# Fourteen early expert products from whole operands, token-by-token one-hots and ten whole closing blocks in a one-core encoder step

## The chip, the core and the metric

The kernel runs on one core of a Trainium2 chip. A core has five engines that run beside each other, each with its own instruction queue: TensorE (PE, matrix products; its weight loads are listed apart as PEld), VectorE (DVE), ScalarE (ACT), GpSimd (POOL) and SyncE (SP, which only issues transfers here). The metric is the device time in microseconds of one execution: the median of several runs.

## The reference, cut to what matters

The program is one layer of an encoder for two groups of tokens that share all weights: 512 prompt tokens and 128 sample tokens, 1024 features each. First comes a mixing part (gated spatial unit, differential attention, gated DeltaNet), then PEER, a retrieval of single-neuron experts. Only PEER is touched:

```
q = (h @ w_query).reshape(n, 8, 2, 128)
s = einsum('nhpd,hpkd->nhpk', q, sub_keys)        # 8 heads, 2 halves, 128 keys each
top_s, top_i = top_k(s, 16)
cand = top_s[:, :, 0, :, None] + top_s[:, :, 1, None, :]
best_s, best_c = top_k(cand.reshape(n, 8, 256), 16)
ids   = i1 * 128 + i2                              # 128 of 16384 experts per token
gates = softmax(best_s)
act = gelu(einsum('nkd,nd->nk', expert_u[ids], h))
out = einsum('nk,nkd->nd', gates * act, expert_v[ids])
x = layer_norm(alpha * x + gate2 * out)
```

## The kernel before

The 640 tokens are five tiles of 128: tiles 0 to 3 are the prompt, tile 4 the samples. The two halves of PEER use the experts in two ways.

Tiles 0 to 2 (384 tokens) go densely through all experts, in 128 blocks of 128 experts. For block n the **u product** is a 128 x 384 table of first products (24 matmuls), ACT makes gelu of it into a tile `ga` (L1539), DVE multiplies it by that block's dense gates `gt` (L1706), and the **v product** adds the block's share of the output into six PSUM banks (18 matmuls). Tiles 3 and 4 fetch the rows of their own experts by indirect DMA, one row per token at a time (512 fetches in all, issued by POOL at L1675), and DVE either dots the row with the token (L1684) or adds it, weighted, into the output (L1690).

Operands are kept in pairs: the value rounded to a shorter type (`uh`, `vh`, `wh`, `h2h`, written by ACT, or by POOL for h) and the remainder (`ul`, `vl`, `wl`, `h2l`, written by DVE). Each product is three passes: high x high, high x low, low x high. Hence 24 = 3 x 8 matmuls in a u product and 18 = 3 x 6 in a v product.

PEER runs in these stages, each of which appears below by its time in the trace:

- the selection of the sample tile, which lies beside the end of the mixing part
- **d_prompt** (660 to 801 us): query products on PE for the 512 prompt tokens, scores, and the two top-16 selections on DVE (L1309 to L1343). Beside it run the u products of blocks 0 to 7 (`prefill`, LEAD = 8), woven in by `lanes`, a merger that takes the next piece of whichever list is least far ahead by the costs that the pieces yield
- **d_decode** (801 to 842 us): DVE turns the selected positions into expert numbers and gates (L1354 to L1389)
- **table** (842 to 990 us): 48 groups of 8 tokens build the dense gates. Per group DVE compares (`ob`, L1612; `o2`, L1615) and multiplies (`o1`, L1616, for five tokens, printed `o`); ACT multiplies the other three (`o1a`, L1614); PE does 8 matmuls into bank `sa`; ACT copies twice into `stg` (L1621), which goes to DRAM (`gdense`)
- the **loop** over m = 0 to 127 (from 990 us): iteration m does the v product of block m and the u product of block n = m + 8, prepares the operands of the next ones, and issues and consumes a share of the fetches that `goal(m)` sets, so that the last one is consumed in iteration END = 118. The order of the work on each queue is as written: `tick` pieces lie between `v_hi`, `g_hi`, `u_split`, `g_lo`, `v_lo`
- the **tail** (from 2051 us): residual, gating and layer norm of the tiles (`base` L1736 and L1739, `final_stats` L1744, `final` L1752 to L1756), placed in iterations 121, 122 and 123 for tiles 3 and 4, and the last three v blocks (LAST = 3), which multiply v by the gate first (L1697) and are added at L1849

## Time and profile before

| | us |
|---|---|
| median of 3 runs | 2128.05 (2126.98 to 2131.91) |
| profiled execution: its own time | 2136.78 |
| profiled execution: span of the trace | 2134.7 |
| PE busy in the span | 1918.1 (90%) |
| DVE busy | 1765.8 (83%) |
| ACT busy | 707.1 (33%) |
| POOL busy | 803.9 (38%) |

The profiled execution took 8.7 us more than the median, 0.4%. In the span's 40 equal slices TensorE's granted clock is 0.9 or full nearly everywhere; from the slice that begins at about 1014 us on, the DMA engines are busy at nine tenths or more until the tail, at 382 to 409 GB/s. Times in the rows below are counted from the start of the span; an item `x8` is a run of eight instructions of one kind, and the time in square brackets is how long the engine stood idle before it and for whom.

### The profile page before, as it was taken

The numbers are of one execution on the slowest core, as the hardware profiler recorded it, in microseconds if no ns is written. First come the engines' busy times: TensorE is split into PE (matmuls) and PEld (weight loads), VectorE is DVE, ScalarE is ACT, GpSimd is POOL, SyncE is SP. The second block draws the span as 40 slices with busy tenths as digits, with TensorE's granted clock in tenths as the row PEclk, the third lists the DMA queues.
The fourth block names the chain that finished last, engine by engine and source line by source line (L and its number), as shares of the span: only waits on it lengthen the run. The fifth ranks groups of instructions, "written<-read, shape, count | busy, mean of one in ns | idle before, by whom it ended". The sixth has DMA issues, their size and how long they took to land.

```text
span 2134.7 us, 32342 instructions
## 1 busy us (share of the span) xinstructions
PE 1918.1 (90%) x11979; PEld 1621.0 (76%) x11979; DVE 1765.8 (83%) x3923; ACT 707.1 (33%) x1257; POOL 803.9 (38%) x637
## 2 busy tenths in 40 slices
PE   5899979988969972999999999999999999999983
PEld 3888956664658871998998888888888888888862
DVE  5753057666898999886999989999999999999987
ACT  2331133332124321886333333333333333333320
POOL 1322122110004201000666666665666666665610
PEclk7999989999989995999999999999999999999986
DMA  7345276523333202567999999999999999999961
GB/s 272 123 177 188 81 237 213 183 93 140 120 136 119 100 20 89 169 189 228 387 409 409 406 382 390 400 399 398 394 399 407 398 408 388 397 395 397 384 235 69
DMA packets 211655, 572.58 MB, mean 268 GB/s; under 512 B 20351, under 2 KB 89471, under 8 KB 206634
## 3 DMA queue, kind: packets, MB, share of 16 engines
q1 hardware_dynamic: 129674, 293.43, 38.0%
q0 software_dynamic: 73728, 268.47, 31.9%
q10 hardware_dynamic: 8096, 8.63, 1.2%
q8 instruction: 94, 1.54, 0.3%
q14 instruction: 63, 0.52, 0.1%
HBM read 535.57 MB, written 34.36 MB: 267 GB/s over the span
## 4 chain that ended last, share of the span: by engine, by line
PE 32%; DVE 21%; issue 18%; POOL 18%; DMA 7%; ACT 3%; ACTq 0%; POOLq 0%; SPq 0%; DVEq 0%
PE mm L188 15%; POOL rows L1675 9%; POOL acc L1675 9%; PE sa L188 7%; PE a L188 3%; PE g L188 3%; ACT uh L243 1%; DVE vl L1702 1%; DMA rows<-in_v_dram,idq 1%; DMA acc<-in_v_dram,ids 1%; DVE acc L1690 1%; DVE acc L1684 1%; DVE ycs L1690 1%; DVE rows L1684 1%; DVE ul L244 1%
## 5 line engine op out<-in xcount | busy, mean ns | idle before, releaser
L1709 ACT CAST wh<-ga 128x384 fp32r<-128x384 f32 x128 | 65.7, 514 | 715.6 <-DVE ga L1706 715.6
L188 PE MATMUL mm<-h2h,uh 128*128 128x384 f32 x1024 | 203.8, 340 | 12.7 <-ACT uh L243 12.2
L188 PEld LDWEIGHTS mm<-h2h,uh 128*128 128x128 f32 x1024 | 179.2, 188 | 35.8 <-ACT uh L243 28.3
L244 DVE TENSOR_TENSOR ul<-ur,uh 128x1024 fp32r<-128x1024 f32 x127 | 155.6, 1225 | 55.5 <-ACT uh L243 55.5
L188 PE MATMUL mm<-h2l,uh 128*128 128x384 f32 x1024 | 199.6, 336 | 0.0
L188 PE MATMUL mm<-h2h,ul 128*128 128x384 f32 x1024 | 199.4, 336 | 0.0
L1675 POOL DMA_INDIRECT acc<-in_u_dram,idq x65 | 83.2, 1280 | 272.3 <-DVE act_q L1684 193.2
L188 PE MATMUL sa<-vl,wh 128*128 128x512 f32 x384 | 160.5, 418 | 25.6 <-DVE vl L1702 25.6
L188 PEld LDWEIGHTS mm<-h2h,ul 128*128 128x128 f32 x1024 | 180.6, 188 | 0.0
L188 PEld LDWEIGHTS mm<-h2l,uh 128*128 128x128 f32 x1024 | 180.5, 187 | 0.0
L188 PE MATMUL sa<-vh,wh 128*128 128x512 f32 x384 | 153.7, 400 | 23.1 <-ACT wh L1709 19.2
L1702 DVE TENSOR_TENSOR vl<-vr,vh 128x1024 fp32r<-128x1024 f32 x128 | 156.2, 1221 | 0.7 <-ACT vh L1699 0.7
L188 PE MATMUL sa<-vh,wl 128*128 128x512 f32 x384 | 152.4, 397 | 0.0
L1699 ACT CAST vh<-vr 128x1024 fp32r<-128x1024 f32 x128 | 133.0, 1039 | 30.3 <-DVE vr L1697 21.4
L243 ACT CAST uh<-ur 128x1024 fp32r<-128x1024 f32 x128 | 133.9, 1047 | 15.2 <-PE mm L188 15.2
L188 PE MATMUL sa<-o,o 128*128 128x128 f32 x480 | 118.7, 408 | 12.2 <-DVE o L1616 12.2
L188 PEld LDWEIGHTS sa<-vl,wh 128*128 128x128 f32 x384 | 73.3, 191 | 61.7 <-DVE vl L1702 49.4
L188 PEld LDWEIGHTS sa<-o,o 128*128 128x128 f32 x480 | 95.2, 209 | 20.7 <-DVE o L1616 12.6
L244 POOL TENSOR_TENSOR wlo<-raw,whi 128x2048 fp32r<-128x2048 f32 (+1 forms) x12 | 55.2, 4597 | 139.8 <-ACT whi L243 108.8
L188 PE MATMUL tp<-vh,wh 128*128 128x512 f32 x256 | 102.2, 399 | 0.0
L188 PE MATMUL tp<-vl,wh 128*128 128x512 f32 x256 | 102.0, 399 | 0.0
L1675 POOL DMA_INDIRECT acc<-in_v_dram,ids x65 | 82.2, 1265 | 52.0 <-DVE ycs L1690 46.2
(474 smaller groups left out, 4688.3 us busy)
## 6 DMA issues: line engine op xcount, KB each, us to landing
ur<-in_uT_dram SPq DMA_DIRECT2D x128, 512.0 KB, 6.7
vr<-in_v_dram SPq DMA_DIRECT2D x128, 512.0 KB, 6.6
raw<-in_wada_dram SPq DMA_DIRECT2D x24, 1024.0 KB, 6.6
gdense<-stg SPq DMA_DIRECT2D x12, 2048.0 KB, 8.7
gt<-gdense SPq DMA_DIRECT2D x31, 768.0 KB, 9.4
ck<-in_ckT_dram SPq DMA_DIRECT2D x32, 512.0 KB, 5.7
cv<-in_cv_dram SPq DMA_DIRECT2D x32, 512.0 KB, 4.5
wqr<-in_wq_dram SPq DMA_DIRECT2D x32, 512.0 KB, 3.2
```

The costliest lines, as they stand in the source:

```text
L188: PE.matmul(out, lhsT=lhsT, rhs=rhs, start=start, stop=stop, **kw)
L243: S.copy(out=hi, in_=raw)
L244: e_lo.tensor_tensor(out=lo, in0=raw, in1=hi.bitcast(F32), op=ALU.subtract)
L1675: G.indirect_dma_start(out=r, out_offset=None, in_=I["v"] if k else I["u"], in_offset=bass.IndirectOffsetOnAxis(ap=who[t][0][:, s:s + 1], ...
L1684: V.tensor_tensor_reduce(out=r, in0=r, in1=h2, scale=1.0, scalar=0.0, op0=ALU.mult, op1=ALU.add, accum_out=act[:, s:s + 1])
L1690: V.scalar_tensor_tensor(out=facc[t], in0=r, scalar=act[:, s:s + 1], in1=facc[t], op0=ALU.mult, op1=ALU.add)
L1699: S.copy(out=vs[n][0], in_=w)
L1702: V.tensor_tensor(out=vs[n][1], in0=vls.pop(n), in1=vs[n][0].bitcast(F32), op=ALU.subtract)
L1709: S.copy(out=ws[n][0], in_=ga)
```

## The change

- **Early u products from whole operands.** NPRE = 14 blocks are now computed ahead of the loop, in the order 8 to 13, then 0 to 7. Eight of them (8 to 13, 0, 1) are woven beside d_decode, six (2 to 7) beside the table; d_prompt runs alone. They use the 32-bit u block and the 32-bit h of tiles 0 to 2 directly (no `uh`/`ul`): 24 matmuls of 128 columns each. For this `h2f` keeps h of the three tiles, copied by DMA into buffers named `acc`, which later serve the fetches. Blocks 8 to 13 store their `ga` to DRAM (`gad`), and iterations 0 to 5 of the loop load them back; those iterations have no u product and no `u_split`. The split of block 14 is done by POOL.
- **One-hots token by token.** `o1` is laid out as 5 rows of 128 instead of 128 rows of 5. PE now reads it contiguously; DVE writes it with a step of 512 bytes between neighbours.
- **Whole operands at the end.** For blocks from WHOLE = 118 on, v and `ga` are used as they are: no `vh`, `vl`, `wh`, `wl`, and 6 matmuls of 512 columns in place of 18.
- **Pacing.** END is 121, `goal` gives the first six iterations half a share of fetches, and `base`/`final` of tiles 3 and 4 lie in iterations 122 to 124.

```diff
@@ -27,6 +27,7 @@
 NP = 512
 ND = 384
 LEAD = 8
+NPRE = 14
 NB = 8
 TS = 16
 PAST = 1024
@@ -1288,11 +1289,16 @@
     cx = ExitStack()
     oc = Out(cx)
 
+    h2f = {}
+
     def h2_tile(t):
         hm = T(oc.p, [P, 8, P], "hm")
         oc.feat(t, hm)
         r = slice(t * P, (t + 1) * P)
         split(hm, h2h[:, :, r], h2l[:, :, r], G)
+        if t < 3:
+            h2f[t] = T(ac, [P, D], "acc", bufs=4)
+            nc.scalar.dma_start(out=h2f[t].rearrange("p (c t) -> p c t", c=8), in_=hm)
         if t == 3:
             for hf in range(2):
                 pt = bank("tp")
@@ -1540,16 +1546,29 @@
 
     uls, uhs, gas = {}, {}, {}
 
-    def prefill():
-        uls[0] = u_load(0)
-        uls[1] = u_load(1)
-        uhs[0] = u_split(uls.pop(0), G)
-        yield 0
-        for n in range(LEAD):
-            uls[n + 2] = u_load(n + 2)
-            uhs[n + 1] = u_split(uls.pop(n + 1), V)
-            u_gelu(n, u_block(n))
-            yield 5
+    gad = T(dp, [NPRE - LEAD, P, ND], "gad")
+    early = list(range(LEAD, NPRE)) + list(range(LEAD))
+
+    def prefill(k0, k1):
+
+        for k in range(k0, k1):
+            n = early[k]
+            if k + 2 < NPRE:
+                uls[early[k + 2]] = u_load(early[k + 2])
+            w = uls.pop(n)
+            gas[n] = T(eu, [P, ND], "ga", bufs=LEAD + 1)
+            pa = bank("mm")
+            for t in range(3):
+                for dc in range(8):
+                    mm(pa[:, t * P:(t + 1) * P], w[:, dc, :], h2f[t][:, dc * P:(dc + 1) * P], dc == 0, dc == 7)
+            u_gelu(n, pa)
+            if n >= LEAD:
+                nc.sync.dma_start(out=gad[n - LEAD], in_=gas.pop(n))
+            yield 5.4
+        if k1 == NPRE:
+            for n in range(NPRE, NPRE + 2):
+                uls[n] = u_load(n)
+            uhs[NPRE] = u_split(uls.pop(NPRE), G)
 
     def d_decode():
         for t in range(4):
@@ -1558,8 +1577,11 @@
         V.scalar_tensor_tensor(out=i1f[:, 3, :], in0=i1f[:, 3, :], scalar=128.0, in1=i2f[:, 3, :], op0=ALU.mult, op1=ALU.add)
         V.tensor_copy(out=idq, in_=i1f[:, 3, :])
 
-    lanes((d_prompt(), 0, 1 / 100.0), (prefill(), 0.3, 1 / 70.0))
-    lanes((d_decode(), 0, 1.0))
+    for q in early[:2]:
+        uls[q] = u_load(q)
+    for _ in d_prompt():
+        pass
+    lanes((d_decode(), 0, 1 / 60.0), (prefill(0, 8), 0, 1 / 40.0))
     dx.close()
 
 
@@ -1606,18 +1628,18 @@
                     col = 32 * c + n0
                     ob = T(tp, [P, P, 8], "ob", BF16, bufs=2)
                     m = TOGETHER
-                    o1 = T(tp, [P, P, m], "o1", bufs=2)
+                    o1 = T(tp, [P, m, P], "o1", bufs=2)
                     o1a = T(tp, [P, 8 - m, P], "o1a", bufs=2)
                     o2 = T(tp, [P, 8, P], "o2", bufs=2)
                     V.tensor_tensor(out=ob, in0=iob8, in1=i1b[:, col:col + 8].unsqueeze(1).to_broadcast([P, P, 8]), op=ALU.is_equal)
                     for n in range(m, 8):
                         S.activation(o1a[:, n - m, :], ob[:, :, n], AF.Copy, scale=sm[:, 1, col + n:col + n + 1])
                     V.tensor_tensor(out=o2, in0=iot, in1=slot(0, col, 8), op=ALU.is_equal)
-                    V.tensor_tensor(out=o1, in0=ob[:, :, 0:m], in1=sm[:, 1, col:col + m].unsqueeze(1).to_broadcast([P, P, m]), op=ALU.mult)
+                    V.tensor_tensor(out=o1.rearrange("p n e -> p e n"), in0=ob[:, :, 0:m], in1=sm[:, 1, col:col + m].unsqueeze(1).to_broadcast([P, P, m]), op=ALU.mult)
                     for q in range(0, 8, 4):
                         pg = bank("sa")
                         for n in range(q, q + 4):
-                            mm(pg.rearrange("p (i n) -> p i n", n=4)[:, :, n - q], o2[:, n, :], o1[:, :, n] if n < m else o1a[:, n - m, :])
+                            mm(pg.rearrange("p (i n) -> p i n", n=4)[:, :, n - q], o2[:, n, :], o1[:, n, :] if n < m else o1a[:, n - m, :])
                         S.copy(out=stg[:, :, n0 + q:n0 + q + 4], in_=pg.rearrange("p (i n) -> p i n", n=4))
                     yield 1
                 nc.sync.dma_start(out=gd_[:, :, 4 * t + c].rearrange("g e i n -> e g (i n)"),
@@ -1629,14 +1651,14 @@
                     nc.sync.dma_start(out=gts[0][:, 0:11], in_=gd_[0, :, 0:11])
         V.tensor_copy(out=gts[0][:, 11], in_=stg[:, 0:4, :])
 
-    for _ in table():
-        pass
+    lanes((table(), 0, 1 / 48.0), (prefill(8, NPRE), 0.05, 1 / 40.0))
     tx.close()
 
 
     NBLK = 128
     LAST = 3
-    END = 118
+    END = 121
+    WHOLE = 118
     ex = ExitStack()
     ep = pool(ex, "ep", side="right")
     gs_q = gates[:, 3, :]
@@ -1695,27 +1717,37 @@
         w = vls[n]
         if n >= NBLK - LAST:
             V.tensor_tensor(out=w, in0=w, in1=fin["p"], op=ALU.mult)
+        if n >= WHOLE:
+            vs[n] = (vls.pop(n),)
+            return
         vs[n] = (T(ep, [P, D], "vh", F32R, bufs=LAST), T(ep, [P, D], "vl", F32R, bufs=LAST)) if n else (first_vh, first_vl)
         S.copy(out=vs[n][0], in_=w)
 
     def v_lo(n):
+        if n >= WHOLE:
+            return
         V.tensor_tensor(out=vs[n][1], in0=vls.pop(n), in1=vs[n][0].bitcast(F32), op=ALU.subtract)
 
     def g_hi(n):
         ga = gas[n]
         V.tensor_tensor(out=ga.rearrange("p (c n) -> p c n", c=12), in0=ga.rearrange("p (c n) -> p c n", c=12),
                         in1=gts[n // 4][:, :, n % 4, :], op=ALU.mult)
+        if n >= WHOLE:
+            ws[n] = (gas.pop(n),)
+            return
         ws[n] = w_pair() if n else first_w
         S.copy(out=ws[n][0], in_=ga)
 
     def g_lo(n):
+        if n >= WHOLE:
+            return
         V.tensor_tensor(out=ws[n][1], in0=gas.pop(n), in1=ws[n][0].bitcast(F32), op=ALU.subtract)
 
     accb = {}
 
     def v_bank(t, hf, ns, first, last):
 
-        todo = [(n, a, b) for n in ns for a, b in ((0, 0), (0, 1), (1, 0))]
+        todo = [(n, a, b) for n in ns for a, b in (((0, 0), (0, 1), (1, 0)) if n < WHOLE else ((0, 0),))]
         for k, (n, a, b) in enumerate(todo):
             mm(accb[t, hf], ws[n][a][:, t * P:(t + 1) * P], vs[n][b][:, hf * 512:hf * 512 + 512],
                first and k == 0, last and k == len(todo) - 1)
@@ -1770,8 +1802,9 @@
             nc.sync.dma_start(out=fin[n], in_=I["lnp"][k:k + 1, :].partition_broadcast(P).rearrange("p a n -> p (a n)"))
 
 
+
     def goal(m):
-        cost = lambda n: 2 * min(n, NBLK - LEAD) + max(0, n - (NBLK - LEAD))
+        cost = lambda n: n + min(max(0, n - (NPRE - LEAD)), NBLK - NPRE)
         return int(len(work) * min(1.0, cost(m + 1) / cost(END)))
 
     mx_ = ExitStack()
@@ -1789,7 +1822,10 @@
         n = m + LEAD
         g0 = goal(m - 1) if m else 0
         part = lambda j: tick(g0 + (goal(m) - g0) * j // 4)
-        if n + 2 < NBLK:
+        if n < NPRE:
+            gas[n] = T(eu, [P, ND], "ga", bufs=LEAD + 1)
+            nc.sync.dma_start(out=gas[n], in_=gad[n - LEAD])
+        elif n + 2 < NBLK:
             uls[n + 2] = u_load(n + 2)
         if m + 2 < NBLK:
             v_load(m + 2)
@@ -1801,7 +1837,7 @@
             v_hi(m + 1)
             g_hi(m + 1)
         part(1)
-        if n + 1 < NBLK:
+        if NPRE < n + 1 < NBLK:
             uhs[n + 1] = u_split(uls.pop(n + 1), V)
         part(2)
         if m + 1 < NBLK:
@@ -1810,13 +1846,13 @@
         if m + 1 < NBLK:
             v_lo(m + 1)
         part(4)
-        if n < NBLK:
+        if NPRE <= n < NBLK:
             pa = u_block(n)
         if m < NB_:
             for t in range(3):
                 for hf in range(2):
                     v_bank(t, hf, [m], m == 0, m == NB_ - 1)
-        if n < NBLK:
+        if NPRE <= n < NBLK:
             u_gelu(n, pa)
         if m == NBLK - LEAD:
             final_rows()
@@ -1825,18 +1861,18 @@
         if m == END:
             while fetched:
                 consume()
-        if m == NBLK - LEAD + 1:
+        if m == END + 1:
             base(3)
             for hf in range(2):
                 final_stats(3, hf)
             x_get(0)
-        if m == NBLK - LEAD + 2:
+        if m == END + 2:
             base(4)
             for hf in range(2):
                 final_stats(4, hf)
             x_get(1)
             final(3)
-        if m == NBLK - LEAD + 3:
+        if m == END + 3:
             final(4)
             x_get(2)
         if m == NB_ - 1:
```

How the queues change, at three places. First PE between the last score matmul of d_prompt (`tp<-keysT,qt`) and the first matmuls of the table (`sa<-o,o`); `cst` is the identity of a transpose. Before:

```order
L188 MATMUL tp_8459<-keysT_5824,qt_8424 128x128 x4
L188 MATMUL mm_9851<-h2h_5805,uh_8238 128x384 x8
L188 MATMUL mm_9851<-h2l_5806,uh_8238 128x384 x8
L188 MATMUL mm_9851<-h2h_5805,ul_8239 128x384 x8
L205 MATMUL tp_8680<-cst_63,i1f_5815 128x128
```

and at the start of the table after; `acc` here is h of a tile, `ur` the whole u block, and rows above these hold eight such blocks in a row behind the last score matmul:

```order
L206 MATMUL tp_8657<-cst_63,gates_5814 128x128
L189 MATMUL mm_8735<-acc_6266,ur_8535 128x128 x8
L189 MATMUL mm_8735<-acc_6534,ur_8535 128x128 x8
L189 MATMUL mm_8735<-acc_6827,ur_8535 128x128 x8
L189 MATMUL mm_8900<-acc_6266,ur_8578 128x128 x8
L189 MATMUL mm_8900<-acc_6534,ur_8578 128x128 x8
L189 MATMUL mm_8900<-acc_6827,ur_8578 128x128 x8
L189 MATMUL sa_8676<-o_1619_8667,o_1621_8669 128x128 x4
L189 MATMUL sa_8682<-o_1619_8667,o_1621_8669 128x128
L189 MATMUL sa_8682<-o1a_8668,o_1621_8669 128x128 x3
L189 MATMUL mm_9085<-acc_6266,ur_8732 128x128 x3
L189 MATMUL sa_8698<-o_1625_8689,o_1627_8691 128x128 x4
```

Eight blocks stand ahead of the table's transposes, two more between them and the first group, and then three matmuls of a block follow each of the first 32 groups.

DVE in the table, one group before:

```order
L1612 TENSOR_TENSOR ob_8711<-iob_1627_8678,i1b_8685 128x1024
L1615 TENSOR_TENSOR o_1641_8714<-cst_63,slots_8684 128x1024
L1616 TENSOR_TENSOR o_1639_8712<-ob_8711,slots_8684 128x640
L1612 TENSOR_TENSOR ob_8733<-iob_1627_8678,i1b_8685 128x1024
L1615 TENSOR_TENSOR o_1647_8736<-cst_63,slots_8684 128x1024
```

and after:

```order
L1634 TENSOR_TENSOR ob_8688<-iob_1613_8655,i1b_8662 128x1024
L1637 TENSOR_TENSOR o_1627_8691<-cst_63,slots_8661 128x1024
L1638 TENSOR_TENSOR o_1625_8689<-ob_8688,slots_8661 128x128x5
L1634 TENSOR_TENSOR ob_8710<-iob_1613_8655,i1b_8662 128x1024
L1637 TENSOR_TENSOR o_1633_8713<-cst_63,slots_8661 128x1024
```

The order is the same; only the pattern of the third operation has become 128 by 5 with a step.

PE at the start of the loop, the end of iteration 0 and the start of iteration 1, before:

```order
L188 MATMUL so_9828<-vh_9799,wh_9797 128x512
L188 MATMUL so_9828<-vl_9804,wh_9797 128x512
L188 MATMUL so_9828<-vh_9799,wl_9798 128x512
L188 MATMUL mm_9919<-h2h_5805,uh_9841 128x384 x8
L188 MATMUL mm_9919<-h2l_5806,uh_9841 128x384 x8
L188 MATMUL mm_9919<-h2h_5805,ul_9842 128x384 x8
L188 MATMUL sa_9823<-vh_9833,wh_9837 128x512
```

and after:

```order
L189 MATMUL so_9983<-vh_9954,wh_9952 128x512
L189 MATMUL so_9983<-vl_9959,wh_9952 128x512
L189 MATMUL so_9983<-vh_9954,wl_9953 128x512
L189 MATMUL sa_9978<-vh_9988,wh_9992 128x512
L189 MATMUL sa_9978<-vl_9989,wh_9992 128x512
L189 MATMUL sa_9978<-vh_9988,wl_9993 128x512
```

The u product is gone from the first six iterations.

## Rows read from the trace of the kernel before

**Rows 1.** Stages: window, length, busy PE, PEld, DVE, ACT, POOL, clock, DMA share, GB/s.

```profile
660.50:801.30 140.80, 128.88 (x670) 113.78 (x668) 131.79 (x805) 43.40 (x58) 30.80 (x13) 0.97 0.20 67
801.30:842.30 41.00, 3.40 (x9) 1.42 (x9) 40.62 (x112) 2.11 (x8) 0.00 (x0) 0.50 0.04 15
842.30:990.20 147.90, 143.70 (x768) 133.20 (x768) 123.14 (x146) 118.64 (x243) 8.12 (x6) 0.97 0.66 193
990.20:2051.40 1061.20, 1022.61 (x5024) 899.08 (x5024) 999.00 (x1249) 337.61 (x485) 636.77 (x506) 1.00 1.01 394
2051.40:2134.70 83.30, 43.76 (x144) 32.20 (x144) 67.59 (x149) 11.30 (x16) 0.00 (x0) 0.71 0.26 98
```

**Rows 2.** DVE groups by line in d_prompt: busy, mean ns, idle before.

```profile
L1309 DVE MAX8 tv<-sc 128x8 f32<-128x128 f32 x64 | 17.0, 282 | 7.7 <-ACT sc L1479 7.7
...
L244 DVE TENSOR_TENSOR ul<-ur,uh 128x1024 fp32r<-128x1024 f32 x7 | 8.5, 1216 | 5.2 <-ACT uh L243 5.2
```

**Rows 3.** PE timeline in the mixing part: start, busy, operation; products of whole operands.

```profile
560.03 1.95 PE L188 MATMUL sa<-h2T,wqr 128*128 128x128 f32 x16
561.82 0.82 PE L205 MATMUL tp<-cst,rr 128*128 128x128 f32 x6
...
567.68 13.04 PE L188 MATMUL mm<-wo,yT 128*128 128x512 f32 x30
580.56 0.38 PE L188 MATMUL sa<-keysT,qts 128*128 128x128 f32 x2
```

**Rows 4.** PE timeline, one group of the table.

```profile
961.69 2.47 PE L188 MATMUL sa<-o,o 128*128 128x128 f32 x10
963.98 0.85 PE L188 MATMUL sa<-o1a,o 128*128 128x128 f32 x6
964.66 2.47 PE L188 MATMUL sa<-o,o 128*128 128x128 f32 x10
```

**Rows 5.** DVE timeline, one group of the table.

```profile
979.73 1.23 DVE L1615 TENSOR_TENSOR o<-cst,slots 128x1024 f32<-128x1024 f32 x1 [0.41 <-PE sa L188]
980.87 0.82 DVE L1616 TENSOR_TENSOR o<-ob,slots 128x640 f32<-128x640 bf16 x1
981.61 0.68 DVE L1612 TENSOR_TENSOR ob<-iob,i1b 128x1024 bf16<-128x1024 bf16 x1
```

**Rows 6.** DVE groups by line and shape in d_decode.

```profile
L1359 DVE TENSOR_TENSOR gates<-e,es 128x128 f32<-128x128 f32 x4 | 1.5, 383 | 0.0
...
L1354 DVE TENSOR_TENSOR e<-bs 128x128 f32<-128x128 f32 x4 | 1.2, 288 | 0.0
...
L1559 DVE CAST idq<-i1f 128x128 uint32<-128x128 f32 x1 | 0.2, 219 | 0.0
```

**Rows 7.** The same view in d_prompt, one strided cast.

```profile
L1338 DVE CAST tib<-ti 128x128 bf16<-128x128 uint32 x8 | 3.6, 446 | 0.0
```

**Rows 8.** One line's instructions from 990 us: the gelu of a block.

```profile
L1539 ACT ACTIVATE ga<-mm x120: 470/482/493, 1001.7 to 2052.4; 128x384 f32<-128x384 f32 x120
```

**Rows 9.** DVE groups by line in the loop, 1100 to 2000 us.

```profile
L244 DVE TENSOR_TENSOR ul<-ur,uh 128x1024 fp32r<-128x1024 f32 x102 | 125.0, 1226 | 35.6 <-ACT uh L243 35.5
```

**Rows 10.** PE timeline: a u product, then the v product behind it.

```profile
1303.87 1.56 PE L188 MATMUL mm<-h2h,uh 128*128 128x384 f32 x8
...
1308.07 0.40 PE L188 MATMUL sa<-vh,wh 128*128 128x512 f32 x1
```

**Rows 11.** DVE timeline, first split of the loop.

```profile
1000.43 1.23 DVE L244 TENSOR_TENSOR ul<-ur,uh 128x1024 fp32r<-128x1024 f32 x1 [6.92 <-ACT uh L243]
```

**Rows 12.** DVE timeline in the tail.

```profile
2051.41 0.55 DVE L1706 TENSOR_TENSOR ga<-ga,gt 128x384 f32<-128x384 f32 x1
...
2054.15 0.55 DVE L1706 TENSOR_TENSOR ga<-ga,gt 128x384 f32<-128x384 f32 x1
...
2084.26 0.55 DVE L1706 TENSOR_TENSOR ga<-ga,gt 128x384 f32<-128x384 f32 x1
...
2087.56 0.68 DVE L1736 TENSOR_TENSOR acc<-sa,gates 128x512 f32<-128x512 f32 x1
```

## The prediction

> **What bounds the kernel now.** I read the stages first, as busy time per stretch, because the change touches five stages with different limits [rows 1]. In d_prompt DVE is busy 131.8 of 140.8 us and PE 128.9: two engines near their limit, DVE ahead. In d_decode it is DVE alone (40.6 of 41.0) while PE does 3.4. In the table PE is busy 143.7 of 147.9 and DVE 123.1. In the loop everything is near full: PE 1022.6, DVE 999.0 of 1061.2, DMA share 1.01 at 394 GB/s. In the tail DVE holds 67.6 of 83.3 us. The timelines of single groups then show who waits. In the table o2 stands 0.41 us idle for PE's `sa` bank [rows 5]; in the loop the only wait of DVE that comes back is the one of `ul` for ACT's `uh`, 35.6 us over 102 blocks [rows 9]; in the tail DVE runs operand after operand [rows 12]. One block of the loop takes (2052.4 - 1001.7) / 119 = 8.83 us [rows 8].
>
> All sums are made against the profiled execution (own time 2136.8: the span of 2134.7 and 2.1 around it) and then taken off the median 2128.05, which lies 0.4% lower; a difference of 0.2%, some 4 us, is about what a measurement of this kernel can tell.
>
> **d_prompt: -13.** The seven `ul` leave DVE: 8.5 us busy; neighbouring DVE operations overlap by 0.08 (0.82 busy, 0.74 from start to start of o1 [rows 5]), so 7 x 1.14 = 8.0. With them goes their wait for ACT, 5.2 [rows 2]. PE loses eight u products of 4.20 (1303.87 to 1308.07 [rows 10]), 33.6 of 128.9, and is left with 95 against DVE's 123, so it cannot become the bound. 8.0 + 5.2 = 13.2. The 7.7 of L1309 for ACT's score copy [rows 2] may shrink too, since PE has time to run ahead; I leave it: -13, at best -16.
>
> **d_decode: 0.** A whole-operand matmul of 128 columns costs (561.82 - 560.03) / 8 = 0.224 us: the 16 records in that stretch are two passes of eight products, by the program. One block is 24 of these, 5.36 us. Eight blocks are 42.9 us on a PE that is busy for 3.4 of DVE's 41.0 [rows 1, 3]; PE also ends d_prompt early, since DVE selects last. What hides them is DVE's decode. New are gelu and exponential taking turns on ACT: I allow 0 to +3 for DVE waiting behind a table load. If the cover were gone, the two blocks that stand in front of the first `sa` would cost 10.7.
>
> **Table: +2.** PE now: five strided o1 matmuls take 961.69 to 963.98, 0.458 each; three contiguous ones 963.98 to 964.66, 0.23 each [rows 4]. The period is 2.97, PE's. With a contiguous o1 PE needs 8 x 0.23 = 1.84, and with three prefill matmuls (0.67) 2.51 in 32 groups, 1.84 in the last 16. DVE without waits needs ob 0.60, o2 1.14, o1 0.74 = 2.48, from start to start [rows 5] (ob is its 0.68 less the overlap). So PE's bound goes, and what is late next is DVE, by whatever the strided write of o1 costs. No row has 512 bytes of step. The nearest: `gates` at L1359 writes with 32 bytes of step in 383 ns where the contiguous `e` at L1354 takes 288 for as many elements [rows 6]: +0.74 ns per element, on 640 elements +0.48, o1 1.22, group 2.96. The strided cast L1338 (16 bytes of step, two-byte results) takes 446 where a contiguous cast L1559 takes 219 [rows 6, 7]: +1.77 ns, o1 1.87, group 3.61. The other end is no penalty, group about 2.5. Over 48 groups against 142.8 (48 x 2.97): -23, -1, +30. I take a group of 3.05, a little above the row of the same type and operation: 146.4, +3.6, less some 2 of PE's lag behind DVE at the table's end: +2. ACT, 118.6 in 147.9 [rows 1], gains six gelus of 0.48 [rows 8] and stays below DVE.
>
> [...]
>
> **Loop: -13.** Up to the last consumed fetch DVE does the same 512 fetches before and after. What differs: `ul` 119 times before (blocks 9 to 127), 113 after (15 to 127): 6 x 1.14 and 6 waits of 0.35 (35.6 / 102 [rows 9]), -8.9. The fetches end in iteration 121 instead of 118, so `ga` three times more (+1.4), while `vl` and `wl` run for blocks 1 to 117 instead of 1 to 119 (-2.3, -0.9). Sum -10.7. At the start DVE stood 6.9 us idle before its first split [rows 11], behind ACT, which waits for a transfer; with no split there, I count 2 of it: -13. PE: six u products less (-25), three v products more, and four of them whole. A 512-column product of whole operands is (580.56 - 567.68) / 15 = 0.859, a whole v product 6 x 0.859 = 5.15 (the 30 records are 15 products), against 4.15 for 18 split matmuls [rows 3, 10]: +16.5. PE thus loses 8.7 of 1022.6 in a loop that gets 13 shorter: 97% busy, tight. DMA: six u loads less, three v loads more, six `ga` reloads: -3.1 + 1.6 + 1.2 MB, next to nothing. So 394 GB/s must become 399 for the -13. Bounds: -14, and 0 where transfers decide. The fetches' buffers are free when the sixth table block is done, a third of the table earlier, so that wait is covered.
>
> **Tail: -17.** Before, eight blocks' operands (120 to 127) are left on DVE: five at 2.74 to 2.80 (2051.41 to 2054.15), three at 3.30 (2084.26 to 2087.56, without the multiplication by the gate) [rows 12], waits for ACT's `wh` included: 23.8. After, blocks 123 to 127 are left with `ga` alone, 5 x 0.47 = 2.4; all the rest of DVE's work in the tail is the same. -21.4. Against it: some 1.5 for loads of v and x that were hidden by the longer queue; PE's six whole products of the last blocks at the low clock (.71 on average there [rows 1]) +0.9; and DVE, running ahead, waits for PE's last v products (5.15 each), some 2. -17, between -12 and -21.
>
> **Sum.** -13 + 0 + 2 - 13 - 17 = -41: 2087 us.
>
> **Rivals.**
> *No penalty on the strided write.* For it: a DVE operation's time in these rows follows its elements (640 in 0.82, 1024 in 1.23). Against: rows 6 and 7. The table gives -23 instead of +2: 2062.
> *The loop is held by transfers.* For it: DMA share 1.01 before any change, no fewer bytes after, 0.35 us of slack per block. Against: DVE's waits name ACT far more than DMA. The loop gives 0: 2100.
> *The strided write decides the table, and the kernel is slower.* The place is L1616 in each of 48 groups, with all three queues of the table behind it. If a four-byte element pays twice what the two-byte cast pays in all (446 / 128 = 3.5 ns), that is 7 ns each: o1 4.5, group 6.2, the table +155 and the time 2240. If it pays 4.5 ns, o1 is 2.9, the group 4.6, +78, 2163. It decides from where the table eats the other 43 us: a group of 2.97 + 43/48 = 3.87, o1 2.13, 3.3 ns per element. Against: no f32 row pays a quarter of that extra.
> *The early blocks aren't hidden.* Gelu behind exponential on ACT, in the order of its queue, holds the two `mm` banks, and the ten blocks ahead of the first `sa` end late: by two blocks, +11: 2098. For it: the exponentials wait for DVE's decode. Against: d_prompt takes 33.6 us off PE and 13 off DVE, so PE comes to these blocks long before DVE comes to decode.
>
> **How the numbers follow.** Forecast 0.50 (2087, own range 2074 to 2102); no penalty 0.23; transfers 0.13; not hidden 0.06; slower 0.06; within 0.2% of before 0.02. The range takes in the no-penalty case with some room, and upward the transfers and half the way to the 1.77 ns end: 2056 to 2108. Faster by over 0.2%: 0.92; within 0.2%: 0.02; slower: 0.06.
>
> **What would show it.** d_prompt near 127 us with PE under 100 busy; d_decode still 41, PE nearly full in it at the high clock. In the table the mean of the o1 line: 0.82 means no penalty, 1.2 to 1.5 my case, over 2.2 a slower kernel; PE's o1 matmuls at 0.23, and DVE's waits for `sa` gone. In the loop the first six iterations near PE's 4.15 to 5 us each and the rest still 8.83; if the rest is slower, or the DMA share stays at 1.01 with long waits of DVE for `rows` and `acc`, the transfers rule it. In the tail no `wl`, `vl` and no waits for `wh`, and 66 us from the last consume to the end. What would make the forecast wrong is above all o1's write and a loop that is not DVE's.

## The result and the profile after

The changed kernel takes 2096.85 us (median of 4 runs, 2092.99 to 2098.68) against 2129.98 for the kernel before measured with it: a ratio of 0.984 (0.982 to 0.986), 33 us less; the forecast was 41 less. The ratios below leave out one execution, which took 7139 us where the others of its kernel took 2083 to 2090. The stages of its profiled execution (span 2096.9), in the columns of [rows 1]:

```profile
658.84:777.00 118.16, 112.58 (x646) 97.55 (x644) 115.97 (x797) 33.07 (x45) 30.00 (x13) 0.99 0.20 69
777.00:818.05 41.05, 35.36 (x291) 35.17 (x291) 40.67 (x111) 14.09 (x20) 0.00 (x0) 0.90 0.33 113
818.05:974.59 156.54, 122.21 (x966) 115.08 (x966) 137.35 (x145) 115.77 (x251) 43.92 (x7) 0.92 0.64 190
974.59:2033.92 1059.33, 1018.50 (x4928) 882.92 (x4928) 990.78 (x1244) 326.63 (x469) 638.01 (x506) 1.00 1.01 396
2033.92:2096.90 62.98, 31.67 (x60) 12.88 (x60) 52.54 (x130) 0.00 (x0) 0.00 (x0) 0.74 0.24 88
```

Marked on DVE by the same instructions in both traces (first selection of d_prompt, first operation of decode, first `ob`, copy of the last gates, last consumed row, end of the span), the stages went as follows.

| stage | before | after | difference | forecast |
|---|---|---|---|---|
| up to the first selection | 660.5 | 658.8 | -1.7 | 0 |
| d_prompt | 140.7 | 118.2 | -22.5 | -13 |
| d_decode | 41.0 | 41.0 | 0 | 0 |
| table | 147.0 | 156.5 | +9.5 | +2 |
| loop to the last consumed row | 1062.2 | 1059.3 | -2.9 | -13 |
| tail | 83.2 | 63.0 | -20.2 | -17 |

The sum, -37.8, is that of two single executions. Only decode came out as forecast. DVE's groups by line in the table (busy, mean ns of one, idle before), to be set against the single operations of [rows 5]:

```profile
L1638 DVE TENSOR_TENSOR o<-ob,slots 128x640 f32<-128x640 bf16 x48 | 62.5, 1302 | 0.0
L1637 DVE TENSOR_TENSOR o<-cst,slots 128x1024 f32<-128x1024 f32 x48 | 59.3, 1236 | 1.9 <-PE sa L189 1.8
L1634 DVE TENSOR_TENSOR ob<-iob,i1b 128x1024 bf16<-128x1024 bf16 x48 | 33.6, 700 | 14.5 <-ACT o1a L1636 14.5
```

o1 costs 1.302 us instead of 0.82. DVE has no gap of 0.41 any more, and a group is 2.83 us (from `o1` to `o1`, 959.15 to 961.98 in its timeline). But in front of one `ob` DVE stood idle for 14.5 us. PE, against [rows 4], a group's two pieces and the three prefill products behind them (two records each):

```profile
836.26 1.35 PE L189 MATMUL sa<-o,o 128*128 128x128 f32 x10 [0.17 <-ACT stg L1643]
837.45 0.83 PE L189 MATMUL sa<-o1a,o 128*128 128x128 f32 x6
838.12 0.83 PE L189 MATMUL mm<-acc,ur 128*128 128x128 f32 x6
```

The five o1 products take 1.19 us, 0.24 each, where they took 0.458.

**The wait of 14.5 us** is read backwards through four queues, by their timelines. DVE waits for ACT's `o1a`, of which there are two buffers:

```profile
906.09 1.27 DVE L1638 TENSOR_TENSOR o<-ob,slots 128x640 f32<-128x640 bf16 x1
921.86 0.69 DVE L1634 TENSOR_TENSOR ob<-iob,i1b 128x1024 bf16<-128x1024 bf16 x1 [14.50 <-ACT o1a L1636]
```

ACT stands for 17.6 us before it may write `stg`, because an earlier store has not left it:

```profile
920.82 0.59 ACT L1643 COPY stg<-sa 128x512 f32<-128x512 f32 x1 [17.61 <-DMA gdense<-stg]
```

The store was issued late. SP had the load of a u block in front of it, and this load waited for a buffer from 878.95 on; it left at 909.46, and the three stores behind it from 909.90 on, one after the other:

```profile
878.95 0.36 SPq L1645 DMA_DIRECT2D gdense<-stg  x1
909.46 0.35 SPq L1523 DMA_DIRECT2D ur<-in_uT_dram  x1
909.90 20.28 SPq L1645 DMA_DIRECT2D gdense<-stg  x3
```

And what it waited for was POOL, which makes the remainder of block 14 (SP's waits, in all, times, longest):

```profile
SPq L1523 <- POOL ul L245: 30.1, 1, 30.1
```

The same operation took POOL 2.43 us in the kernel before, just ahead of d_prompt:

```profile
651.30 2.43 POOL L244 TENSOR_TENSOR ul<-ur,uh 128x1024 fp32r<-128x1024 f32 x1
```

Here it lasts 29.49, and ends 2.1 us after DVE has stopped, about what it takes by itself:

```profile
879.95 29.49 POOL L245 TENSOR_TENSOR ul<-ur,uh 128x1024 fp32r<-128x1024 f32 x1 [142.22 <-ACT uh L244]
909.61 1.15 POOL L1697 DMA_INDIRECT acc<-in_u_dram,idq  x1 [0.17 <-issue]
```

At the end of the loop DVE waits for fetched rows, 10.2 us in all (four of the lines):

```profile
2022.34 1.28 DVE L1712 SCALAR_TENSOR_TENSOR ycs<-rows,act_s,ycs 128x1024 f32<-128x1024 f32 x1 [3.39 <-DMA rows<-in_v_dram,ids]
2024.89 1.28 DVE L1712 SCALAR_TENSOR_TENSOR ycs<-rows,act_s,ycs 128x1024 f32<-128x1024 f32 x1 [1.27 <-DMA rows<-in_v_dram,ids]
...
2030.01 1.28 DVE L1712 SCALAR_TENSOR_TENSOR ycs<-acc,act_s,ycs 128x1024 f32<-128x1024 f32 x1 [1.27 <-DMA acc<-in_v_dram,ids]
2032.64 1.28 DVE L1712 SCALAR_TENSOR_TENSOR ycs<-acc,act_s,ycs 128x1024 f32<-128x1024 f32 x1 [1.35 <-DMA acc<-in_v_dram,ids]
```

### The profile page after: what moved, and what is told of

Its sections match the earlier page's. It is cut to its first block, busy times and chain, and to the rows that moved or that the text cites. A ratio compares the mean times of both kernels' runs of the same rounds, so it can differ in the third digit from the quotient of the medians.

```text
span 2096.9 us, 32846 instructions
## 1 busy us (share of the span) xinstructions
PE 1898.2 (91%) x12255; PEld 1587.4 (76%) x12255; DVE 1737.9 (83%) x3889; ACT 682.2 (33%) x1229; POOL 837.5 (40%) x637
## 4 chain that ended last, share of the span: by engine, by line
DVE 26%; PE 21%; POOL 21%; issue 19%; DMA 9%; ACT 2%; ACTq 0%; POOLq 0%; SPq 0%; DVEq 0%
PE mm L189 11%; POOL rows L1697 10%; POOL acc L1697 9%; PE a L189 3%; PE g L189 3%; DMA acc<-in_v_dram,ids 2%; DVE o L1638 2%; DVE acc L1712 2%; DVE o L1637 2%; POOL ul L245 1%; DMA acc<-in_v_dram,idq 1%; DVE rest L1318 1%; DMA rows<-in_v_dram,ids 1%; PE ad L189 1%; DVE ycs L1712 1%
## 5 line engine op out<-in xcount | busy, mean ns | idle before, releaser
L189 PE MATMUL mm<-h2h,uh 128*128 128x384 f32 x912 | 181.9, 341 | 8.8 <-ACT uh L244 8.1
L189 PEld LDWEIGHTS mm<-h2h,uh 128*128 128x128 f32 x912 | 159.7, 188 | 30.2 <-ACT uh L244 23.1
L189 PE MATMUL mm<-h2l,uh 128*128 128x384 f32 x912 | 177.7, 336 | 0.0
L189 PE MATMUL mm<-h2h,ul 128*128 128x384 f32 x912 | 177.5, 336 | 0.0
L189 PEld LDWEIGHTS mm<-h2h,ul 128*128 128x128 f32 x912 | 160.7, 188 | 0.0
L189 PEld LDWEIGHTS mm<-h2l,uh 128*128 128x128 f32 x912 | 160.7, 187 | 0.0
L1697 POOL DMA_INDIRECT rows<-in_u_dram,ids x65 | 84.0, 1293 | 50.3 <-DVE act_s L1706 46.3
L1697 POOL DMA_INDIRECT acc<-in_v_dram,idq x64 | 80.1, 1251 | 51.9 <-DVE acc L1712 46.7
L1697 POOL DMA_INDIRECT rows<-in_u_dram,idq x63 | 82.7, 1313 | 45.2 <-DVE act_q L1706 41.5
L1697 POOL DMA_INDIRECT rows<-in_v_dram,idq x64 | 80.7, 1260 | 50.0 <-DVE acc L1712 39.9
```

The lines of the kernel that those rows point to most:

```text
L189: PE.matmul(out, lhsT=lhsT, rhs=rhs, start=start, stop=stop, **kw)
L1697: G.indirect_dma_start(out=r, out_offset=None, in_=I["v"] if k else I["u"], in_offset=bass.IndirectOffsetOnAxis(ap=who[t][0][:, s:s + 1], ...
```

## The experiments

Four questions were open: whether that chain explains the table, what each of the parts brings alone, why d_prompt gained so much, and what held POOL. Where a stretch of two kernels is compared below, it is that of their profiled executions.

**Block 14 split on DVE.** The last statement of `prefill` goes, and iteration 5 does the split:

```diff
-            uhs[NPRE] = u_split(uls.pop(NPRE), G)
...
-        if NPRE < n + 1 < NBLK:
+        if NPRE <= n + 1 < NBLK:
```

> The changed kernel, but block 14 is split in iteration 5 of the loop, its remainder on DVE instead of on POOL beside the table. Theory: POOL's 29.5 us for that one remainder held a u load on SP, behind it the stores of the table, and so ACT (17.6 us) and DVE (14.5 us). Then the wait of 14.5 us on DVE in the table is gone, POOL's remainder is not there, and the time falls by 12 to 15 us from the changed kernel's 2096.9, to about 2083. Rival: the stores themselves are slow beside the u loads; then ACT still waits over 10 us for a store and the time stays within 4 us of 2097.

Measured: 2086.8 us (2076.8 to 2096.1), ratio 0.981 (0.977 to 0.984). The wait is gone and the table takes 140.3 us instead of 156.5: the chain is shown. The time is 10 us below that of the changed kernel, less than the 12 to 15 expected, and the intervals of the two ratios overlap. For 13 of the 16 us come back in the first eight iterations (from the copy of the last gates to the gates of block 8, 55.4 us instead of 42.5). Now it is the first fetch on POOL that lasts 52 us, until DVE has done its last group at 949.95, and all six are issued in six microseconds:

```profile
898.89 51.96 POOL L1696 DMA_INDIRECT acc<-in_u_dram,idq  x1 [166.57 <-DVE o L1637]
951.15 0.94 POOL L1696 DMA_INDIRECT acc<-in_u_dram,idq  x1 [0.30 <-issue]
...
956.13 0.94 POOL L1696 DMA_INDIRECT rows<-in_u_dram,idq  x1 [0.30 <-issue]
```

The last store of the table is issued at 952.76 beside them. The load that waits for it goes out 19 us later, where the changed kernel needed 9.3 (974.58 to 983.85):

```profile
952.76 0.36 SPq L1644 DMA_DIRECT2D gdense<-stg  x1
972.05 0.33 SPq L1593 DMA_DIRECT2D gt<-gdense  x1
```

DVE pays at the first gates and at the second `wl`: there ACT's rounding of v, ahead of its `wh`, stands 10.7 us until the store has landed.

```profile
960.21 0.56 DVE L1732 TENSOR_TENSOR ga<-ga,gt 128x384 f32<-128x384 f32 x1 [5.27 <-DMA gt<-gdense]
...
973.54 0.56 DVE L1743 TENSOR_TENSOR wl<-ga,wh 128x384 fp32r<-128x384 f32 x1 [11.17 <-ACT wh L1738]
```

**The layout of o1 alone**, in the kernel before:

```diff
-                    o1 = T(tp, [P, P, m], "o1", bufs=2)
+                    o1 = T(tp, [P, m, P], "o1", bufs=2)
```

(with the write and PE's read turned accordingly).

> The kernel before with the token-by-token layout of o1 alone. Theory: PE's o1 matmuls fall from 0.458 to 0.23, the strided write makes DVE's o1 1.30 us busy (from 0.82), the table goes from PE's 2.97 a group to DVE's 2.83, so about -7 us: 2123. Rival: DVE's write was paid only because PE's prefill matmuls ran beside it; then o1 stays near 0.82, the group falls to 2.5 and the time to about 2107.

Measured: 2122.7 us, ratio 0.9966 (0.9948 to 0.9984), and the table 139.6 us instead of 147.0. The write has its price without any prefill beside it:

```profile
L1616 DVE TENSOR_TENSOR o<-ob,slots 128x640 f32<-128x640 bf16 x48 | 61.9, 1290 | 0.0
```

**Whole operands at the end alone**: `WHOLE = 118` and its branches in the kernel before, END left at 118.

> The kernel before with whole operands in the last ten blocks alone (its last fetch still in iteration 118). Theory: the shorter tail comes from the vl, wl and their waits that DVE no longer does: from the last fetch to the end 83 us become 63 to 65, about -19 us, 2110. Rival: it came from moving the closing work of tiles 3 and 4 and the last fetch by three iterations; then less than 8 us are gained, 2122 or more.

Measured: 2114.4 us, ratio 0.993 (0.991 to 0.995). From the multiplication of block 118's gates to the end of the span it is 92.9 us instead of 105.7, -12.8: less than expected, more than the rival allowed. The changed kernel needs 106.0 for the same stretch. So the 20 us of its tail are not a gain of that size: three more iterations with fetches and their waits lie in front of the mark, and what the whole operands brought in this stretch is taken up again there (no run changes END alone). By blocks, which END doesn't move, the time from the copy of the last gates to the end falls from 1145.4 to 1122.3 us, and nearly all of it in the first eight iterations (64.7 to 42.5); the next 110 blocks take 975.1 and 973.9, the rest 105.7 and 106.0.

**Eight early blocks.** The changed kernel with

```diff
-NPRE = 14
+NPRE = 8
...
-            uhs[NPRE] = u_split(uls.pop(NPRE), G)
+            uhs[NPRE] = u_split(uls.pop(NPRE), V)
...
-    lanes((table(), 0, 1 / 48.0), (prefill(8, NPRE), 0.05, 1 / 40.0))
+    for _ in table():
+        pass
```

> The changed kernel with eight early blocks only (none beside the table, none kept in DRAM; block 8 is split on DVE). Theory: d_prompt keeps its 22 us, the tail its 20, the table runs at 2.83 a group without the wait of 14.5 us, but the first six iterations cost 8.4 to 9.4 us each again instead of 4.4, so that the loop is some 20 us longer: about 2097, the same as the changed kernel. Rival: the six early blocks bring nothing, because transfers limit the loop; then the time is 2080 to 2085.

Measured: 2082.2 us (2080.3 to 2088.3), ratio 0.979 (0.976 to 0.981): the rival's number, though not shown to be for its reason, and better than the changed kernel. The first eight iterations are long again (65.4 us), as the theory had it. But the table is at 139.8, and the next 110 blocks take 959.5 us instead of 973.9: `goal` spreads the same fetches over 241 units instead of 235, so that POOL issues 468 there instead of 479, and DVE is busy 913.8 us instead of 927.3. From the copy of the last gates to the end it takes 1126.3 us, against 1127.1 with six more early blocks and the split on DVE, and 1122.3 in the changed kernel.

**Fetches held back**, on top of the split on DVE: the fetches read a copy of the indices that DVE makes behind the first multiplication by the gates.

```diff
+    idq2 = T(ep, [P, P], "idq2", U32)
...
+    V.tensor_copy(out=idq2, in_=idq)
```

> The kernel with block 14 split in the loop, and the first six fetches of the prompt tile held back until DVE has the table's last gates (they read a copy of the indices that DVE makes there). Theory: beside the table POOL's first fetch took 52 us and all six were then issued at once with the last store, whose landing took 19 us instead of 9; with them behind it the store lands in 9 us again, the loop's first gates are multiplied 2 to 3 us after the copy of the last gates instead of 7, the second at 9 instead of 21, and the time falls by 7 to 10 us against the same kernel without the hold, to 2072 to 2078. Rival: the store is slow for another reason, or the fetches are missed in the first iterations; then the time does not fall by more than 3 us.

Measured: 2089.9 us, ratio 0.983 (0.980 to 0.986). The local part holds: the store lands in 9.5 us again.

```profile
953.58 0.36 SPq L1644 DMA_DIRECT2D gdense<-stg  x1
963.12 0.33 SPq L1593 DMA_DIRECT2D gt<-gdense  x1
```

The total doesn't fall. The 3 MB of the six fetches now run beside the first loads of v; ACT's rounding stands 10.83 us until one of these has landed, and DVE waits behind it, 10 us at the fourth `wl`:

```profile
956.80 0.56 DVE L1744 TENSOR_TENSOR wl<-ga,wh 128x384 fp32r<-128x384 f32 x1 [0.44 <-ACT wh L1739]
...
979.64 0.56 DVE L1744 TENSOR_TENSOR wl<-ga,wh 128x384 fp32r<-128x384 f32 x1 [10.12 <-ACT wh L1739]
```

**Closing loads late**, on top of the held fetches: `x_get` of tiles 3 and 4 and `final_rows` are issued by POOL in iteration END.

```diff
-        if m == NBLK - LEAD:
-            final_rows()
-            x_get(3)
-            x_get(4)
         if m == END:
+            x_get(3, G)
+            x_get(4, G)
+            final_rows(G)
```

> As the one with held fetches, and the four loads of the closing work (x of tiles 3 and 4, the two rows of the layer norm) are issued by POOL behind the last fetch instead of by SP two iterations earlier. Theory: DVE's 10 us of waits for fetched rows at the end of the loop come from these 2.6 MB in front of the last fetches; then from block 118 to the last consumed row it takes 35 us instead of 40, and some 3 to 5 us are left of it in the total. Rival: it is the fetches' own number in short iterations that waits; then the stretch stays at 40 us and the closing work starts later, total 0 to +6 us.

Measured: 2085.2 us (2082.6 to 2089.5), ratio 0.980 (0.977 to 0.984). The stretch from block 118 to the last consumed row takes 37.8 us instead of 40.5, half of what the theory wanted, and the total is the same within the intervals. Inconclusive: these loads may be part of the waits, and are not all of them.

**POOL beside the table**, a first pair: eight multiplications of 128x256 on POOL in group 16, in the kernel before and in the one with the layout alone.

```diff
+                    if (t, c, n0) == (1, 0, 0):
...
+                        for _ in range(8):
+                            G.tensor_tensor(out=prb, in0=sm, in1=sm, op=ALU.mult)
```

> The kernel before with eight added POOL multiplications of 128x256 (0.8 us each elsewhere in the trace) that wait for group 16 of the table, the first six fetches between them on POOL's queue. In this table DVE stands 0.41 us idle in each group. Theory (POOL gets in only where DVE stands idle): each operation of POOL takes at most one group, 1 to 3.5 us, and all of them are done within 14 groups. Rival (POOL's 29.5 us were a matter of that one operation): the same durations here and in the kernel with the token-by-token layout.

> The same eight POOL multiplications and six fetches in the kernel before with the token-by-token layout of o1 alone, where DVE runs its table groups without a gap. Theory: POOL is shut out; one or more of its operations take 20 to 60 us, and the rest are done only after the last group of the table. Rival: durations as in the kernel before, at most 3.5 us each.

In both kernels the operations ran from the end of decode through the first five or six groups, since what they wait for is made early; multiplications took 0.62 to 0.83 us each and fetches 1.25 to 1.79. So nothing is shut out at the start of the table, and the question of its middle needed another pair, whose multiplications read a copy of `stg` that ACT makes in group 24:

```diff
+                    if (t, c, n0) == (1, 2, 0):
...
+                        S.copy(out=prs, in_=stg[:, 0:64, 0:4])
+                        for _ in range(8):
+                            G.tensor_tensor(out=prb, in0=prs, in1=prs, op=ALU.mult)
```

> The kernel before, with the eight POOL multiplications of 128x256 now made to wait for a copy that ACT makes in the middle of the table (group 24 of 48), and the first six fetches behind them on POOL's queue. DVE stands 0.41 us idle in each group here. Theory (in the settled table POOL gets in only where DVE stands idle): the eight and the six are done within 14 groups, at most 3 us each. Rival (the long durations of POOL have nothing to do with DVE's gaps): the same as in the dense table.

> The same late multiplications and fetches in the kernel before with the token-by-token layout of o1 alone, where DVE has no gap. Theory: in the middle of the table POOL is shut out; one multiplication takes 10 us or more, at worst to the table's end some 66 us later. Rival: at most 3 us each, as at the start of the table, where the probe of the first kind took 0.62 to 1.79 us in both kernels; then the shut-out needs something that only the changed kernel has beside its table (the whole-operand products on PE, the loads of u).

The fetches ran ahead of them at the start again, 1.0 to 1.9 us each. The eight multiplications are one item of the timeline. In the kernel before, with its gap in each group:

```profile
919.75 9.32 POOL L1626 TENSOR_TENSOR prb<-prs 128x256 f32<-128x256 f32 x8 [68.95 <-ACT prs L1624]
```

and in the dense table, where one of the early fetches stands above them:

```profile
842.03 1.41 POOL L1680 DMA_INDIRECT rows<-in_u_dram,idq  x1 [0.30 <-issue]
907.73 68.12 POOL L1626 TENSOR_TENSOR prb<-prs 128x256 f32<-128x256 f32 x8 [64.29 <-ACT prs L1624]
```

9.3 against 68.1 us, from 907.7 to 975.9; DVE's last group ends at 969.7 there, and the 6.2 us behind it are what eight such multiplications took above, so that hardly any of the eight was done before. With no prefill in either kernel, neither the early products nor their loads are needed for this: the dense table is enough. The two kernels differ in DVE's gap, in its strided write and in PE's reading at once, and no run separates these.

Nor does a dense stream always do it. In the changed kernel, after the wait of 14.5 us, POOL issued fetches one to a group, 2.83 us apart, while DVE ran groups with the same write and without a gap (`o2` from 941.01, 943.84, 946.68 and 949.51):

```profile
941.60 2.53 POOL L1697 DMA_INDIRECT rows<-in_u_dram,idq  x1 [0.30 <-issue]
944.43 2.52 POOL L1697 DMA_INDIRECT rows<-in_u_dram,idq  x1 [0.30 <-issue]
947.26 2.52 POOL L1697 DMA_INDIRECT rows<-in_u_dram,idq  x1 [0.30 <-issue]
```

What decides whether POOL gets in, there and during the first groups, where DVE is as dense, stays open.

**Query weights in quarters**: POOL makes each remainder `wql` of the kernel before in four operations.

```diff
-        split(w, hi, lo, G)
+        S.copy(out=hi, in_=w)
+        for h in (slice(0, 2), slice(2, 4), slice(4, 6), slice(6, 8)):
+            G.tensor_tensor(out=lo[:, h], in0=w[:, h], in1=hi[:, h].bitcast(F32), op=ALU.subtract)
```

> The kernel before, with POOL's remainder of each query weight (2.4 us) made in four pieces of 0.6 us or so. Theory: five of the eight additions cand 128x64 on DVE stood 2 us behind a whole piece of POOL's work; behind a quarter they stand at most 0.6, their mean falls from 1475 ns to under 700, and d_prompt on DVE (from its first selection to the first operation of decode) from 140.7 to 134 to 137 us. Rival: the long additions are long for another reason; then the mean stays over 1200 ns and d_prompt at 140 to 141.

One addition of d_prompt, `cand` 128x64, took 1475 ns on average before and 669 after the change; in the quarters 453 (three kernels, the same view):

```profile
L1342 DVE TENSOR_TENSOR cand<-tv 128x64 f32<-128x64 f32 x8 | 11.8, 1475 | 0.0
```

```profile
L1348 DVE TENSOR_TENSOR cand<-tv 128x64 f32<-128x64 f32 x8 | 5.4, 669 | 0.0
```

```profile
L1342 DVE TENSOR_TENSOR cand<-tv 128x64 f32<-128x64 f32 x8 | 3.6, 453 | 0.0
```

The long ones lie under an operation of POOL and end with it: the one at 672.23 of the kernel before ends at 674.54, POOL's `wql` at 674.47. Five of eight do so before, two of eight after. This part of the theory holds, and the other falls: d_prompt remains at 140.7 us. The additions lose 8.2 us; the casts behind them gain 3.3 of it, since six of the eight now last 1.0 us ([rows 7] has 446 ns). DVE is busy 127.1 us instead of the 131.8 of [rows 1] (the second line, for the stage):

```profile
L1338 DVE CAST tib<-ti 128x128 bf16<-128x128 uint32 x8 | 6.9, 867 | 0.0
```

```profile
659.60:800.30 140.70, 128.88 (x670) 113.92 (x668) 127.06 (x804) 43.37 (x59) 36.18 (x51) 0.97 0.20 68
```

What DVE saved it waits. Of the 13.6 us in the next line 9.1 lie ahead of the stage's first selection, as 4.9 of the 7.7 of [rows 2] do; within the stage DVE's waits grow from 8.0 to 12.4:

```profile
DVE tv L1309 <- ACT sc L1481: 13.6, 7, 9.1
DVE ul L244 <- ACT uh L243: 7.9, 3, 3.3
```

So DVE was not d_prompt's bound. PE was: in the kernel before it is busy without a pause, at a granted clock of 1.00, until its last scores are done.

```profile
660.50:785.20 124.70, 124.70 (x647) 109.92 (x646) 115.72 (x686) 41.52 (x56) 30.80 (x13) 1.00 0.22 76
```

```profile
783.17 2.05 PE L188 MATMUL tp<-keysT,qt 128*128 128x128 f32 x16
```

After the change they are done 90.9 us behind the stage's start instead of 124.7:

```profile
747.66 2.05 PE L189 MATMUL tp<-keysT,qt 128*128 128x128 f32 x16
```

**Eight early blocks, four tokens on DVE**: `TOGETHER = 4` instead of 5.

> The kernel with eight early blocks, and in each group of the table four tokens' o1 on DVE and four on ACT instead of five and three. Theory: the strided write is paid per element (1.11 us from start to start for 640), so 128 fewer save 0.22 a group on DVE and ACT, at about 2.7 a group, becomes the bound: the table goes from 139.8 to 130 to 134 us, the total to 2073 to 2077 from 2082. Rival: ACT's turn with the copies of the banks delays PE, and the table stays or grows: 2080 or more.

Measured: 2077.5 us (2075.5 to 2081.0), ratio 0.973 (0.970 to 0.976): faster than both kernels. The table falls from 139.8 to 130.2 us. DVE still sets its pace, with a group of 2.62 us and 0.7 us of waits for `sa` in all; ACT, busy 123.9 us from 812 to 946 against DVE's 133.0, did not become the bound. The o1 of DVE and of ACT:

```profile
L1638 DVE TENSOR_TENSOR o<-ob,slots 128x512 f32<-128x512 bf16 x48 | 50.7, 1057 | 0.0
```

```profile
L1636 ACT ACTIVATE o1a<-ob,slots 128x128 f32<-128x128 bf16 x192 | 101.7, 631 | 15.4 <-DVE ob L1634 15.4
```

## Why the prediction was right, and where it was not

The time lies within the range, and the gain is 33 us where 41 were forecast. Its terms were further off than their sum, and that the sum came so near is in part luck: by the stages, d_prompt and the tail gave 9.5 and 3 us more than forecast, the table and the loop 7.5 and 10 less.

- **d_prompt, -13.** The step "two engines near their limit, DVE ahead" failed. I compared busy shares, and PE's idle time lies all at the stage's end: the trace of before shows no wait of PE there, its last scores end at 785.2, and DVE selects for 16 us more. Until then PE sets the pace, and DVE's waits (8.0 us; of the 7.7 for scores that I read in the rows, 4.9 lie ahead of the stage) and its additions under POOL's work (6.4 us more than after) cost next to nothing, as the quarters show. With 33.6 us off PE, its last scores end at 749.7, and DVE, 116.0 busy of 118.2, becomes the bound: the gain is the distance down to DVE's own floor, 22.5, more than the `ul` and their waits.
- **d_decode, 0** held: 41.05 us with PE at 35.4 busy. With gelu and exponential in turn, seven ACT_TABLE_LOAD of 1.28 us each stand on ACT in the stage, and DVE has no wait in it.
- **Table, +2.** That the strided write pays, and DVE takes over from PE, was right; o1 is 1.11 from start to start, below the 1.22 worked out from the row of 32 bytes and the 1.31 that the forecast group of 3.05 holds. (48 x 2.97 is 142.6 and not 142.8, which changes nothing.) The layout alone is -7. The term missed what the added work does on other queues: I had looked at PE and ACT for cover, and not at SP, where a load stood in front of the stores, nor at POOL, whose remainder of block 14 the term puts at nothing: 2.43 us before, 29.49 here. That is what the wait of 14.5 us hangs on.
- **Loop, -13.** The sum of DVE's work was right: 999.3 us busy before, 990.8 after, -8.5. But its idle time grew by 5.6: the waits for ACT's `uh` fell by 12.2 us (4 were forecast), those for `wh` at the start rose by 9.4 and those for fetched rows by 7.9, to 17.0, of which 10.2 fall in the last iterations. Of the rivals, that of the transfers is the one that came partly true, at the loop's two ends and not along it. The six blocks beside the table bring nothing measurable once the table's wait is gone, as the run with eight shows. Of the 23 us that they take off the first eight iterations (42.5 against 65.4), 13 are lost again once the table runs without its wait (55.4), to transfers that are late, and the other 10 return in the next 110 blocks, which have more fetches to consume (969.5 against 959.5).
- **Tail, -17**: 63.0 instead of 83.2, and 66 forecast. This size is right, but the mark moved with END; the whole operands themselves are worth 13 us in the trace and 15 in the medians.

The rivals "no penalty" and "slower" are out: o1 at 1.30 and not 0.82 or over 2.2. So is "not hidden": DVE waits 1.8 us for `sa` in the whole table.

## What to carry to other kernels

Before the work of a stage is summed, ask which engine has no wait in it: the other's waits are slack, and what a removal brings goes down to the other's floor (in d_prompt 22.5 us, where the sum gave 13). A change that fills an engine's last gaps may cost another engine time: here, with DVE's 0.41 us a group gone and its write and PE's reading changed along with it, POOL's remainder took 29.49 us where it had taken 2.43 before, and through a buffer that reached SP, the stores and ACT. A queue that mixes loads waiting for buffers with stores that others wait for is to be read row by row before a load is put into it: SP's three stores left here from 0.44 us behind a load that had waited 30.1.

## What the runs showed of the hardware that was not expected

A POOL operation of 2.43 us lasted 29.49 beside the dense table, a fetch of 1 to 2 us lasted 51.96, and eight multiplications 68.1 instead of 9.3, though other fetches took 2.5 us each beside the same dense groups; the other way round a DVE addition of 0.21 us lasted 2.31 under a POOL operation and ended 0.07 behind it (the one at 672.23 of the kernel before). POOL's operation had begun 0.16 us before that addition. Under the POOL operation of 29.49 us DVE was busy 27.41 of the 27.45 us up to its stop, and under the eight multiplications it went on with the table, 64 operations in its timeline from 908.85 to 969.70. What lets the one of the two run and holds the other is not shown by these runs.

The five-token write of o1, 32-bit with 512 bytes of step, took DVE 0.37 us more on 640 elements than the contiguous one (1.11 for 0.74 from start to start), 0.58 ns each; the mean of its line was 1.302 us in the changed kernel, 1.290 with the layout alone, 1.314 with the split on DVE, 1.333 with eight early blocks and 1.289 beside the late multiplications.
